# A decoder layer on one core: the last gate cells in a fixed order, their last products by column halves, the last rows' scaling and stores rearranged

## The chip, the core and the metric

The kernel runs on one core of one Trainium2 chip. The metric is device time in microseconds of that core; the time of a kernel is the median of its runs.

## The reference, cut to what matters

One layer of a hybrid decoder (gated linear attention, a short gated convolution, a merge), then a per-layer embedding gate and a final RMSNorm, on 1024 rows of 1024 columns in float32. What the change touches is the end:

```
x = x + merged @ w_out
ple_gate = sigmoid(rms_norm(x, norm_ple_g) @ w_ple_gate)
x = x + ple_gate * (p @ w_ple_proj)
return rms_norm(x, norm_final_g)
```

`rms_norm(x, g)` is `x / sqrt(mean(x*x) + EPS) * g`, row by row. The last line needs the sum of squares of a whole row before any of that row can be scaled.

## The kernel before, in words

**Products.** Every large product is a Strassen-Winograd product on 2x2 quarters, seven products, numbered 0 to 6, for an output of 256 rows by 1024 columns. A `Cell` computes such an output, as two row blocks of 128 rows by two column halves of 512 columns. Each product has four k-tiles of three matmuls (high x high, low x high, high x low parts in fp32r), so 12 matmuls with 512 columns. A cell has three PSUM banks, X, V and Y. Products 0 and 3 go to X, 1 and 5 to V, 2, 4 and 6 to Y (Y begins as a copy of X after product 0). X after product 3 is the output of row block 0, columns 0 to 511; V after product 5 plus a copy of Y after product 2 is row block 0, columns 512 to 1023; Y after product 4 plus a copy of V after product 1 is row block 1, columns 512 to 1023; Y after product 6 is row block 1, columns 0 to 511. `Cell.run(k)` does one product and hands finished quarters to `cons(i, j, src)`, with i the row block and j the column half.

**The last stage.** Four gate cells, gt0 to gt3, one for each pair of row blocks; gt2 makes rows 4 and 5 of eight, gt3 rows 6 and 7. `run_groups(pairs(gts))` lets two cells alternate product by product in the order 0, 1, 2, 3, 5, 4, 6 (`PAIR`); the right-hand sides wg0 to wg6 are resident, and the left-hand operands are sums and differences of tiles loaded from DRAM (`gt2raw` and so on), split into a high part by an ACT cast and a low part by a DVE subtraction. For a finished quarter, `cons` or `piece` does: ACT sigmoid with the row's factor `rg` as scale; DVE product with the quarter's `pe` tile (p @ w_ple_proj, loaded from DRAM); DVE sum onto `x`; ACT square with the row sum as second output (`junk`, then ACT reads the accumulator). When a row's two halves are there, POOL adds the sums and raises them to the power -1/2 (`rf`), and the row is scaled by `rf` and by the gain `gf` (tile `gfin`, the gain broadcast over the partitions) and stored.

**How rows were finished.** Rows 0 to 4 and row 6 go through `cons`: one DVE pass over 1024 columns with factor and gain, one store of 512 KB. Rows 5 and 7 go through `piece` (lines 1671 to 1700): each quarter is multiplied by the gain when its square sum is under way, POOL adds the partial sums (`pre`), and the last piece takes factor and gain together; two stores of 256 KB. For gt3 the last product, 6, is done by column halves (`last_product`, lines 770 to 783): Y is copied to a free bank Z, the first 256 columns are finished in Y, the others in Z, so that the first half's sigmoid runs during the second half's matmuls.

**What sets the order.** `Flow` (lines 257 to 505) records every operation instead of issuing it. `note` gives each a planned cost by engine and size and links it to what it depends on; `set_dues` gives due times; `put_in_order` makes one sequence, in which PE's matmuls keep the order in which they were recorded and the other engines' operations are placed by due time. `emit` issues them all from line 503, which is why every row of the profile says L503; the tiles' names tell the operations apart. Each engine works its own sequence in order, and waits by semaphores for the others. All DMAs are issued by SP.

Of the kernel before, what the change touches and what calls it, by code (L numbers as in the profile page):

```python
# [9 lines left out]
F32 = mybir.dt.float32  # L10
# [246 lines left out]
class Flow:  # L257
# [5 lines left out]
    def __init__(self, tc):  # L263
        nc = tc.nc
        self.tc, self.ops, self.side, self.open, self.hurry, self.bundle = tc, [], True, [], 0.0, None
        self.tensor, self.vector, self.scalar = Port(self, PE, nc.tensor), Port(self, DVE, nc.vector), Port(self, ACT, nc.scalar)
        self.gpsimd, self.sync = Port(self, POOL, nc.gpsimd), Port(self, SP, nc.sync)


    def note(self, engine, op, call, args, kw):  # L270
# [39 lines left out]

# [28 lines left out]
        for v in outs + ins:  # L339
            if isinstance(v, View) and v.buf not in o.bufs:  # L340
# [174 lines left out]
def kernel(  # L515
# [210 lines left out]
    class Cell:  # L726


        def __init__(self, name, side, src, res, cons, prods=ORDER, begin=None, s1=None, u2=None, s5=None, fresh=(), mixed=False):
# [3 lines left out]
            self.s1, self.seed, self.ready, self.halves = s1, None, lambda k: True, None  # L733
            self.raw, self.ring = [None] * 4, {}
            self.steps, self.fresh = ring_steps(name, side, self.raw, fresh, mixed), fresh
# [33 lines left out]

        def last_product(self):  # L770

            other = psm.tile([P, 512], F32, tag=f"m{3 * (1 - self.set)}", name=f"{self.name}Z")
            nc.scalar.copy(other, self.Y)
            self.prep(6)
            shi, slo = self.ring[6]
            rhi, rlo = self.res[6]
            for n, acc in enumerate((self.Y, other)):
                cs = slice(n * 256, n * 256 + 256)
                for kt in range(4):
                    nc.side = False  # L780
                    mm3(acc[:, cs], shi[:, kt, :], slo[:, kt, :], rhi[:, kt, cs], rlo[:, kt, cs], False, kt == 3)
                    nc.side = True
                self.halves(n, acc[:, cs])

        def run(self, k):
# [16 lines left out]
            elif k == 2:  # L802
                self.product(2, self.Y, False)
                self.c12 = self.taken("u2", self.Y)
            elif k == 3:
                self.product(3, self.X, False)
                self.cons(0, 0, self.X)
            elif k == 5:
                self.product(5, self.V, False)
                tt(self.c12, self.V, self.c12, op=ALU.add)  # L810
                self.cons(0, 1, self.c12)
            elif k == 4:
# [3 lines left out]
            elif k == 6 and self.halves:  # L816
                self.last_product()
# [6 lines left out]
    def line_up(groups):  # L824
        for n, g in enumerate(groups):
            for s, c in enumerate(g):
                c.set = (s if len(g) > 1 else n) % 2
        return [(c, k) for g in groups for k in g[0].prods for c in g]

# [774 lines left out]
    with phase("late", [ph["sw"], ep]) as lp:  # L1604
# [56 lines left out]
        with phase("fin", [ph["sw4"]], lp) as gp:  # L1661
# [3 lines left out]
            def make_gate(p, cell):  # L1665
                seen = [0, 0]
                xt, ms, ts, sums = [], [], [None, None], [None, None]

                def piece(i, cs, src, n, done):
                    w = cs.stop - cs.start
                    a = cs.start
                    if a % 512 == 0:
                        ts[i] = gp.tile([P, 512], F32, tag="pe", name=f"pe{p}_{i}_{a}", bufs=4)
                        load(ts[i], ped[2 * p + i][:, a:a + 512])
                    t, xc = ts[i][:, a % 512:a % 512 + w], xt[i][:, cs]
                    act(src, src, AF.Sigmoid, scale=rgate[p, i][:, 0:1])
                    tt(t, src, t, op=ALU.mult)
                    tt(xc, xc, t, op=ALU.add)  # L1680
                    m = gp.tile([P, 1], F32, tag="msl", name=f"msl{p}_{i}_{n}", bufs=4)
                    act(junk[:, 0:w], xc, AF.Square, scale=1.0 / 32.0, accum_out=m)
                    if not done:
                        tt(xc, xc, gf[:, cs], op=ALU.mult)
                        pre = gp.tile([P, 1], F32, tag="pre", name=f"pre{p}_{i}_{n}", bufs=4)
                        nc.gpsimd.tensor_scalar(pre, m, EPS if n == 0 else sums[i][:, 0:1], None, op0=ALU.add)
                        sums[i] = pre
                        return
                    r = sm.tile([P, 1], F32, tag="rstd", name=f"rf{p}_{i}", bufs=4)
                    nc.gpsimd.tensor_scalar(r, m, sums[i][:, 0:1], None, op0=ALU.add)  # L1690
                    nc.gpsimd.tensor_tensor(r, r, mhalf, op=ALU.pow)
                    if a:
                        act(xt[i][:, 512:], xt[i][:, 512:], AF.Copy, scale=r[:, 0:1])
                    else:
                        nc.vector.tensor_scalar(xt[i][:, 512:], xt[i][:, 512:], r[:, 0:1], None, op0=ALU.mult)
                    store(out[rows(2 * p + i), 512:], xt[i][:, 512:])
                    stt(xc, xc, r[:, 0:1], gf[:, cs], op0=ALU.mult, op1=ALU.mult)
                    if a:
                        nc.vector.tensor_scalar(xt[i][:, 0:a], xt[i][:, 0:a], r[:, 0:1], None, op0=ALU.mult)
                    store(out[rows(2 * p + i), 0:512], xt[i][:, 0:512])  # L1700

                def late_cons(i, j, src):
                    if not xt:
                        get()
                    piece(i, slice(512 * j, 512 * j + 512), src, 1 - j, j == 0)

                def halves(n, src):
                    piece(1, slice(256 * n, 256 * n + 256), src, 1 + n, n == 1)

# [102 lines left out]
```

## Time and profile before

| | us |
|---|---|
| median of 3 runs (lowest to highest) | 1082.56 (1082.08 to 1082.73) |
| the profiled execution | 1082.53 |
| its span, first to last instruction | 1080.4 |
| around the span | 2.13 |
| PE busy | 1069.0 |
| start of the last matmul | 1070.26 |
| issue of the last store | 1077.24 |

The mean granted TensorE clock was 0.997. Times in the profile count from the span's start. A row of the timeline gives start, duration, engine, line, operation, output tile <- input tiles, shapes, a count, and in brackets how long the engine had been idle and what released it. PEld is the weight load beside the matmuls, SPq the sequencer of SP that issues DMAs.

### The profile page before, as it was taken

How to read it: one execution, taken by the hardware profiler on the slowest of the kernel's cores; microseconds unless marked ns; L12 is line 12 of the kernel's file. 1: busy time of each engine (PE TensorE's matmuls, PEld its weight loads, DVE VectorE, ACT ScalarE, POOL GpSimd, SP SyncE). 2: the span in 40 equal slices, each digit the busy share in tenths (PEclk: the TensorE clock that was granted, in tenths of full speed). 3: DMA queues.
4: the chain of work that ended last, by engine and by line, in shares of the span. 5: the costliest groups of instructions: out<-in, count | busy, mean ns of one | idle time of the engine just before them, and what ended most of it. 6: DMA issues, size and time to landing. Idle time of an engine off the chain costs nothing.

```text
span 1080.4 us, 14620 instructions
## 1 busy us (share of the span) xinstructions
PE 1069.0 (99%) x4869; PEld 889.4 (82%) x4869; DVE 868.7 (80%) x1341; ACT 602.6 (56%) x1086; POOL 49.2 (5%) x89
## 2 busy tenths in 40 slices
PE   9999999999999999999999999999999999999996
PEld 7887887888888888888888888888888888888885
DVE  6998567679987977857747788887999879889886
ACT  6778538656543455433343367765756635467554
POOL 0000000000000000000000012110000000012013
PEclk9999999999999999999999999999999999999998
DMA  9973564467866597221222779989586779799954
GB/s 324 347 244 105 178 210 136 148 204 231 233 204 222 202 314 260 77 89 49 88 69 69 249 259 326 326 288 334 201 306 214 282 224 313 233 335 326 319 188 156
DMA packets 144827, 239.95 MB, mean 222 GB/s; under 512 B 12016, under 2 KB 57328, under 8 KB 141808
## 3 DMA queue, kind: packets, MB, share of 16 engines
q1 hardware_dynamic: 144752, 239.02, 65.4%
q8 instruction: 38, 0.62, 0.2%
q14 instruction: 37, 0.30, 0.1%
HBM read 158.24 MB, written 80.74 MB: 221 GB/s over the span
## 4 chain that ended last, share of the span: by engine, by line
PE 97%; DVE 1%; ACT 1%; issue 0%; POOL 0%; POOLq 0%; DVEq 0%; ACTq 0%
PE vY L503 3%; PE zaY L503 3%; PE pe L503 2%; PE vX L503 2%; PE zaV L503 2%; PE vV L503 2%; PE op L503 2%; PE zaX L503 2%; PE kv L503 1%; PE ga2Y L503 1%; PE ga0Y L503 1%; PE ga1Y L503 1%; PE cb3Y L503 1%; PE gc1Y L503 1%; PE ga3Y L503 1%; PE gc0Y L503 1%
## 5 line engine op out<-in xcount | busy, mean ns | idle before, releaser
L503 ACT ACTIVATE junk<-x 128x512 bf16<-128x512 f32 (+1 forms) x29 | 17.9, 616 | 18.9 <-DVE x L503 13.9
L503 ACT ACT_TABLE_LOAD x20 | 25.7, 1283 | 1.1 <-PEq L1801 0.7
L503 DVE TENSOR_TENSOR wt<-wt 128x512 f32<-128x512 f32 x32 | 21.6, 685 | 0.3
L503 POOL MEMSET t<- 128x2 f32 x8 | 0.8, 100 | 442.6 <-DMA qkd<-kk 243.7
L503 DVE SCALAR_TENSOR_TENSOR u<-t,vec,u 128x1024 f32<-128x1024 f32 x16 | 20.4, 1281 | 0.0
L503 POOL TENSOR_SCALAR rg<-ms 128x1 f32<-128x1 f32 x8 | 6.6, 822 | 261.2 <-ACT junk L503 261.0
L503 ACT CAST S<-S 128x512 fp32r<-128x512 f32 x14 | 8.7, 619 | 10.0 <-PE op L503 10.0
L503 ACT ACTIVATE og<-op,or 128x256 f32<-128x256 f32 x32 | 13.3, 469 | 1.6 <-POOL or L503 1.6
L503 ACT ACTIVATE oq<-oq,vec 128x512 f32<-128x512 f32 x20 | 13.3, 715 | 0.0
L503 ACT ACTIVATE junk<-op 128x256 bf16<-128x256 f32 x32 | 12.2, 380 | 1.7 <-PE op L503 1.5
L503 PE MATMUL pe<-wpehi,pThi 128*128 128x512 f32 x32 | 12.8, 401 | 0.0
L503 PE MATMUL op<-v,aTh 128*128 128x256 f32 x64 | 12.8, 283 | 0.0
L503 PE MATMUL pe<-wpelo,pThi 128*128 128x512 f32 x32 | 12.8, 399 | 0.0
L503 POOL TENSOR_TENSOR or<-or,mhalf 128x2 f32<-128x2 f32 x16 | 12.7, 795 | 1.3
L503 PE MATMUL pe<-wpehi,pTlo 128*128 128x512 f32 x32 | 12.6, 394 | 0.0
L503 DVE TENSOR_TENSOR szl<-og,szl 128x512 f32<-128x512 f32 x16 | 11.0, 686 | 1.7 <-ACT og L503 1.7
L503 DVE SCALAR_TENSOR_TENSOR S<-S,dds,kv 128x256 f32<-128x256 f32 x24 | 10.4, 475 | 1.9 <-PE kv L503 1.7
L503 DVE SCALAR_TENSOR_TENSOR hq<-hq,vec,rt 128x512 f32<-128x512 f32 x16 | 11.1, 741 | 0.5 <-PE rt L503 0.5
L503 DVE STREAM_TRANSPOSE oT<-szl 128x512 f32<-128x512 f32 x16 | 11.3, 706 | 0.2
L503 DVE TENSOR_TENSOR u<-u,s 128x512 f32<-128x512 f32 x16 | 10.9, 687 | 0.3
L503 DVE TENSOR_TENSOR x<-x,pe 128x512 f32<-128x512 f32 (+1 forms) x17 | 11.0, 656 | 0.2
L503 DVE SCALAR_TENSOR_TENSOR x<-x,rf,gfin 128x1024 f32<-128x1024 f32 (+2 forms) x8 | 8.9, 1114 | 2.7 <-POOL rf L503 2.7
(2908 smaller groups left out, 4103.0 us busy)
## 6 DMA issues: line engine op xcount, KB each, us to landing
wtd<-wt SPq DMA_DIRECT2D x44, 256.0 KB, 3.7
wt<-in_wb_dram SPq DMA_DIRECT2D x8, 1024.0 KB, 7.2
v<-vd SPq DMA_DIRECT2D x16, 512.0 KB, 5.8
wgq<-wtd SPq DMA_DIRECT2D x7, 1024.0 KB, 8.0
qk<-qkd SPq DMA_DIRECT2D x12, 512.0 KB, 5.9
vraw<-in_wv_dram SPq DMA_DIRECT2D x20, 256.0 KB, 4.0
zaraw<-in_wv_dram SPq DMA_DIRECT2D x20, 256.0 KB, 4.0
uq<-ud SPq DMA_DIRECT2D x5, 1024.0 KB, 7.8
```

The source lines that it names most:

```text
L503: o.call(*[place(a) for a in o.args], **{k: place(a) for k, a in o.kw.items()})
```

## The change

1. The planner's cost of an ACT operation with a row sum grows from 0.1 to 0.2 us over a plain one; a DMA issued by an engine other than SP gets a cost of its own. This changes no operation, but the order that the planner makes, in the whole kernel.
2. A new field `hold` makes recorded operations wait, in the plan, for a given earlier operation; `hurry` gives the last quarters' operations an earlier due time.
3. The order of the last two cells' products is written out: gt2's 0, gt3's 0, then gt2: 3, 1, 2; gt3: 3; gt2: 4; gt3: 1; gt2: 5; gt3: 2; gt2: 6; gt3: 5, 4, 6.
4. `by_halves` replaces `last_product`: gt3's products 4 and 6 are both done by column halves, in Y and Z. Z is filled by a copy of half of Y after product 2. Half products of 4 and 6 go through `piece` in four pieces of 256 columns.
5. All of gt2's and gt3's quarters go through `piece`. Rows 4 and 5: each quarter is multiplied by the gain beside its square sum, the row is scaled by two ACT passes and stored whole. Row 6: the same by halves, with two stores; the second gain product and the ACT scaling are held behind steps of row 7. Row 7: its four square sums land in one tile of five columns, `last`, preset to EPS; one DVE reduction adds them, POOL does the power alone; one gain product stands ahead of the reduction, three behind it; then ACT scales columns 512 to 1023 and DVE columns 0 to 511.
6. The partial sums of rows are added by DVE instead of POOL.
7. Row 7's second half is stored by a DMA that ACT issues; all other DMAs stay with SP.

The diff, cut to its core:

```diff
-            o.cost = 0.10 + n * 0.000833 + (0.1 if "accum_out" in kw else 0.0)
+            o.cost = 0.10 + n * 0.000833 + (0.2 if "accum_out" in kw else 0.0)
...
+        if op == "dma_start" and engine != SP:
+            o.cost, o.lat = 0.1, 2.3 + shape[0] * n * 4 / 250e3
...
+        if self.hold is not None:
+            preds[self.hold] = max(preds.get(self.hold, 0.0), 0.0 if self.ops[self.hold].engine == engine else 0.08)
...
-        def last_product(self):
-            other = psm.tile([P, 512], F32, tag=f"m{3 * (1 - self.set)}", name=f"{self.name}Z")
-            nc.scalar.copy(other, self.Y)
-            self.prep(6)
...
+        def by_halves(self, k):
+            self.prep(k)
+            shi, slo = self.ring[k]
+            rhi, rlo = self.res[k]
+            for n, acc in enumerate((self.Y, self.Z)):
                 cs = slice(n * 256, n * 256 + 256)
                 for kt in range(4):
                     nc.side = False
                     mm3(acc[:, cs], shi[:, kt, :], slo[:, kt, :], rhi[:, kt, cs], rlo[:, kt, cs], False, kt == 3)
                     nc.side = True
-                self.halves(n, acc[:, cs])
+                if k == 4:
+                    tt(self.c22[:, cs], acc[:, cs], self.c22[:, cs], op=ALU.add)
+                    self.halves(1, n, self.c22[:, cs])
+                else:
+                    self.halves(0, n, acc[:, cs])
...
                 self.c12 = self.taken("u2", self.Y)
+                if self.halves:
+                    self.Z = psm.tile([P, 512], F32, tag=f"m{3 * (1 - self.set)}", name=f"{self.name}Z")
+                    nc.scalar.copy(self.Z[:, 256:], self.Y[:, 256:])
...
+                    if p == 3 and i:
+                        if not times:
+                            sums[1] = gp.tile([P, 5], F32, tag="last", name="last")
+                            nc.gpsimd.memset(sums[1], EPS)
+                        m = sums[1][:, n:n + 1]
...
+                    if p == 3 and i:
+                        times.append((cs, t, added))
+                        if not done:
+                            return
+                        nc.vector.tensor_reduce(pre, sums[1], mybir.AxisListType.X, ALU.add)
+                        summed = len(nc.ops) - 1
+                    else:
+                        if p < 3 or not done:
+                            tt(xc, xc, gf[:, cs], op=ALU.mult)
+                        nc.vector.tensor_scalar(pre, m, EPS if n == 0 else sums[i][:, 0:1], None, op0=ALU.add)
                         sums[i] = pre
...
+                    for n, (cs, to, _) in enumerate(times if done else ()):
+                        nc.hold = (times[2][2], summed)[n] if n < 2 else len(nc.ops) - 1
+                        tt(to, xt[i][:, cs], gf[:, cs], op=ALU.mult)
+                    nc.hold = None
+                    if done:
+                        r = sm.tile([P, 1], F32, tag="rstd", name=f"rf{p}_{i}", bufs=4)
+                        nc.gpsimd.tensor_tensor(r, pre, mhalf, op=ALU.pow)
+                        if p == 3 and i == 0:
+                            rest.append(r)
+                            return
+                        if p < 3:
+                            for b in (0, 512):
+                                act(xt[i][:, b:b + 512], xt[i][:, b:b + 512], AF.Copy, scale=r[:, 0:1])
+                            store(out[rows(2 * p + i), :], xt[i])
+                            return
+                        act(xt[1][:, 512:], ts[1, 1], AF.Copy, scale=r[:, 0:1])
+                        nc.vector.tensor_scalar(xt[1][:, 0:512], ts[1, 0], r[:, 0:1], None, op0=ALU.mult)
+                        store(out[rows(7), 0:512], xt[1][:, 0:512])
+                        nc.scalar.dma_start(out[rows(7), 512:], xt[1][:, 512:])
+                        for q, late in enumerate((made, squared)):
+                            js = slice(512 * q, 512 * q + 512)
+                            xj = xt[0][:, js]
+                            if q:
+                                nc.hold = added
+                                tt(xj, xj, gf[:, js], op=ALU.mult)
+                            nc.hold = late
+                            act(xj, xj, AF.Copy, scale=rest[0][:, 0:1])
+                            nc.hold = None
+                            store(out[rows(6), js], xj)
...
+                def halves(j, n, src):
+                    a = 512 * j + 256 * n
+                    nc.hurry = 1.0
+                    piece(1, slice(a, a + 256), src, 2 * (1 - j) + n, a == 256)
+                    nc.hurry = 0.0
...
-                    if i == 1 and p >= 2:
+                    if p >= 2:
                         return late_cons(i, j, src)
...
-            run_groups(pairs(gts))
+            last = pairs(gts)
+            gts[2].order = [(0, 0), (1, 0), (0, 3), (0, 1), (0, 2), (1, 3), (0, 4), (1, 1),
+                            (0, 5), (1, 2), (0, 6), (1, 5), (1, 4), (1, 6)]
+            run_groups(last)
```

More of the change, by code (lines that the diff above doesn't have):

```diff
@@ L733, in __init__ @@
             self.s1, self.seed, self.ready, self.halves = s1, None, lambda k: True, None
-            self.raw, self.ring = [None] * 4, {}
+            self.raw, self.ring, self.order = [None] * 4, {}, None
             self.steps, self.fresh = ring_steps(name, side, self.raw, fresh, mixed), fresh
@@ L811, in run @@
                 self.cons(0, 1, self.c12)
+            elif k in (4, 6) and self.halves:
+                self.by_halves(k)
             elif k == 4:
@@ L827, in line_up @@
                 c.set = (s if len(g) > 1 else n) % 2
-        return [(c, k) for g in groups for k in g[0].prods for c in g]
+        return [(g[s], k) for g in groups
+                for s, k in (g[0].order or [(s, k) for k in g[0].prods for s in range(len(g))])]
     def single(cs):
@@ L1678, in piece @@
                     act(src, src, AF.Sigmoid, scale=rgate[p, i][:, 0:1])
+                    made = len(nc.ops) - 1
                     tt(t, src, t, op=ALU.mult)
                     tt(xc, xc, t, op=ALU.add)
-                    m = gp.tile([P, 1], F32, tag="msl", name=f"msl{p}_{i}_{n}", bufs=4)
-                    act(junk[:, 0:w], xc, AF.Square, scale=1.0 / 32.0, accum_out=m)
[L1683 to L1686, printed above, removed]
-                        sums[i] = pre
-                        return
@@ L1689, in piece @@
[L1689 to L1700, printed above, removed]
+                    added = len(nc.ops) - 1
+                    if p == 3 and i:
[4 more added lines that the diff above has]
+                    else:
+                        m = gp.tile([P, 1], F32, tag="msl", name=f"msl{p}_{i}_{n}", bufs=4)
```

23 lines of the change are left out of this document (10 added, 13 removed).

## The prediction, made before the result

> **What bounds the kernel now.** I read the page first (its first part), then the list of waits of PE, then busy time by stretch:
>
> ```profile
> PE 1069.0 (99%) x4869; PEld 889.4 (82%) x4869; DVE 868.7 (80%) x1341; ACT 602.6 (56%) x1086; POOL 49.2 (5%) x89
> ```
> ```profile
> PE warm L503 <- DVE zero L503: 1.4, 1, 1.4
> ```
> ```profile
> core 0 of [0], span 1080.4 us
> core 0: us, PE busy (x) PEld busy (x) DVE busy (x) ACT busy (x) POOL busy (x), PEclk, DMA share, GB/s
> 1032.00:1060.00 28.00, 28.00 (x125) 23.21 (x124) 20.53 (x30) 13.12 (x27) 3.33 (x4) 1.00 0.54 197
> 1060.00:1070.50 10.50, 10.50 (x58) 9.02 (x56) 9.41 (x15) 6.74 (x15) 3.75 (x5) 1.00 0.50 175
> 1070.50:1080.40 9.90, 0.04 (x1) 0.00 (x0) 4.97 (x11) 3.11 (x10) 4.87 (x6) 0.72 0.28 106
> ```
>
> PE waits once, 1.4 us at the start, and is then busy without a gap until 1070.5 us: 1069.0 + 1.4 + 9.9 makes the span. So three things can change the time: more or fewer matmuls, a wait of PE, and the 9.9 us in which PE has finished and the last rows are still normalized and stored. The timeline of that tail, by engine: PE (first and last matmul of gt2's product 5, then the last of each half of gt3's product 6), ACT, DVE, POOL and SP's queue:
>
> ```profile
> 1053.91 0.39 PE L503 MATMUL gt2V<-wg5hi,gt2hi 128*128 128x512 f32 x1
> ```
> ```profile
> 1056.40 0.39 PE L503 MATMUL gt2V<-wg5hi,gt2lo 128*128 128x512 f32 x1
> ```
> ```profile
> 1068.82 0.28 PE L503 MATMUL gt3Y<-wg6hi,gt3lo 128*128 128x256 f32 x1
> ```
> ```profile
> 1070.26 0.28 PE L503 MATMUL gt3Z<-wg6hi,gt3lo 128*128 128x256 f32 x1
> ```
> ```profile
> 1070.80 0.43 ACT L503 ACTIVATE gt3Z<-gt3Z,rg 128x256 f32<-128x256 f32 x1
> 1071.16 0.62 ACT L503 ACTIVATE junk<-x 128x512 bf16<-128x512 f32 x1
> 1071.68 0.19 ACT L503 ACTIVATION_READ_ACCUMULATOR junk<-x 128x1 f32 x1
> 1071.90 0.42 ACT L503 ACTIVATE junk<-x 128x256 bf16<-128x256 f32 x1
> 1072.23 0.19 ACT L503 ACTIVATION_READ_ACCUMULATOR junk<-x 128x1 f32 x1
> 1073.35 0.42 ACT L503 ACTIVATE junk<-x 128x256 bf16<-128x256 f32 x1 [0.93 <-DVE x L503]
> 1073.67 0.19 ACT L503 ACTIVATION_READ_ACCUMULATOR junk<-x 128x1 f32 x1
> 1076.07 0.72 ACT L503 ACTIVATE x<-x,rf 128x512 f32<-128x512 f32 x1 [2.21 <-POOL rf L503]
> ```
> ```profile
> 1071.87 0.42 DVE L503 TENSOR_TENSOR pe<-gt3Z,pe 128x256 f32<-128x256 f32 x1
> 1072.20 0.69 DVE L503 TENSOR_TENSOR x<-x,gfin 128x512 f32<-128x512 f32 x1
> 1072.80 0.43 DVE L503 TENSOR_TENSOR x<-x,pe 128x256 f32<-128x256 f32 x1
> 1073.14 0.43 DVE L503 TENSOR_TENSOR x<-x,gfin 128x256 f32<-128x256 f32 x1
> 1074.45 0.49 DVE L503 TENSOR_SCALAR x<-x,rf 128x512 f32<-128x512 f32 x1 [0.89 <-POOL rf L503]
> ```
> ```profile
> 1072.12 1.51 POOL L503 TENSOR_SCALAR rf<-msl,pre 128x1 f32<-128x1 f32 x1
> 1073.61 0.28 POOL L503 TENSOR_SCALAR pre<-msl,pre 128x1 f32<-128x1 f32 x1
> 1073.85 0.56 POOL L503 TENSOR_TENSOR rf<-rf,mhalf 128x1 f32<-128x1 f32 x1
> 1074.41 0.57 POOL L503 TENSOR_SCALAR rf<-msl,pre 128x1 f32<-128x1 f32 x1
> 1075.06 0.97 POOL L503 TENSOR_TENSOR rf<-rf,mhalf 128x1 f32<-128x1 f32 x1
> ```
> ```profile
> 1076.81 0.81 SPq L503 DMA_DIRECT2D out_dram<-x  x2
> ```
>
> From the last matmul's start (1070.26, my zero) the last row goes through sigmoid, product with pe, sum onto x, square sum, POOL add, POOL power, scaling, store. Three places lose time. Z's product stands behind others on DVE (sigmoid done at 1071.23, product at 1071.87). A gf product of another row (1072.20) delays the sum onto x to 1072.80. And POOL is late: the last square sum is read by 1073.86, but POOL takes row 5's power first (1073.85), adds row 7's sum at 1074.41, and its power lasts until 1076.03. The first store of the last pair leaves at 1076.81, **6.55 us** after zero; 3.59 us later the span ends.
>
> **The change part by part.** Its own time is the profiled execution's, 1082.53 us: span 1080.4 and 2.13 around it, 0.03 under the median of the runs. Positions come from comparing the instruction order of both programs.
>
> *Matmuls.* Product 4 of gt3 is 24 matmuls of 256 columns in place of 12 of 512. Twelve starts of 512 take (1056.40 - 1053.91)/11 = 0.226 us each, those of 256 (1070.26 - 1068.82)/12 = 0.12. 24 x 0.12 - 12 x 0.226 = **+0.15 us**, all on PE, which nothing hides.
>
> *Fixed order.* gt2's products 3 and 4 come 10.9 us earlier, gt2's 6 and gt3's 3 come 5.4 earlier, gt3's 1 and 2 come 10.9 later. Their operands are split by one ACT cast and one DVE subtraction each. The raw tiles are loaded well before (rival 4), so I take 0. The tightest place is new: gt3's product 6 may not write its first half before DVE has read product 4's. The chain to it is told by gt2's add behind its product 5:
>
> ```profile
> 1056.83 0.69 DVE L503 TENSOR_TENSOR gt2u<-gt2V,gt2u 128x512 f32<-128x512 f32 x1 [1.10 <-PE gt2V L503]
> ```
>
> The last matmul of gt3's product 5 starts at -5.87 (47 x 0.12 + 0.226 back). DVE's add starts 0.43 later (1056.40 to 1056.83) and lasts 0.69, until -4.75; sigmoid 0.72 (the scaling's row), pe product 0.60 from start to start (1072.20 to 1072.80), half add 0.42, and 0.03 at each of two handovers: -2.95. PE wants it at -2.76 (23 x 0.12). 0.2 us of cover: 0 taken, up to 0.3 in the range.
>
> *Planner cost of squares, hurry, hold.* They change no instruction, but reorder ACT, DVE, SP and a few PE instructions all through the kernel (groups of 1 to 3 matmuls change places in four stretches). PE has no gap to lose there: 0 taken; for the range -0.1 to +0.4, a quarter of the one wait that the trace shows (an estimate).
>
> *Sums.* Seven POOL adds go; six 128x1 adds and one 128x5 reduction come to DVE, none shown in that size or form. The nearest rows are ACT's 128x1 read of 0.19 and, above, DVE's 256-wide product of 0.42; below, nothing. I take 0.19. Only the reduction is on the path.
>
> *Rows 4 to 6.* Row 4's 1.28 us pass on DVE becomes two gf products there and two ACT scalings of 0.72; rows 5 and 6 likewise. ACT pays for it: it was busy 6.74 of 10.5 us before the end and is now nearly full. Row 5's factor: DVE adds gt3u until -4.75, then come that sum and a 512 gf product, until -4.0, and POOL's power runs beside the product. How a power fares there, and how ACT's 512-wide passes follow each other, is told by
>
> ```profile
> 999.24 0.69 DVE L503 TENSOR_TENSOR gt0S<-gt0raw,gt0raw 128x512 f32<-128x512 f32 x1
> 999.84 0.69 DVE L503 TENSOR_TENSOR gt1S<-gt1raw,gt1raw 128x512 f32<-128x512 f32 x1
> ```
> ```profile
> 999.49 0.85 POOL L503 TENSOR_TENSOR rg<-rg,mhalf 128x1 f32<-128x1 f32 x1
> ```
> ```profile
> 1067.21 0.71 ACT L503 ACTIVATE gt3s<-gt3s,rg 128x512 f32<-128x512 f32 x1
> 1067.82 0.64 ACT L503 ACTIVATE gt2Y<-gt2Y,rg 128x512 f32<-128x512 f32 x1
> ```
>
> The power, 0.56 alone (1073.85), ended here 0.41 after the DVE operation that it met (999.93), though another followed at once. So row 5's factor comes at -3.6. From there ACT is packed: three 512 scalings at 0.61 (1067.21 to 1067.82), four 256 sigmoids at 0.36 (1070.80 to 1071.16), one 512 square at 0.74 (1071.16 to 1071.90), three 256 squares at 0.53 (256 columns, 0.21, less), the last with its read 0.51 (1073.35 to 1073.86): 1.83 + 1.44 + 0.74 + 1.59 + 0.51 = 6.1, and 0.1 for handovers (1073.23 to 1073.35): 6.2. The last square is in at **+2.6**, against +3.6 before. Beyond ACT's queue stand row 6's scaling, which waits for its own factor (DVE sum at about -1, power by 0), and both squares behind it.
>
> *Behind the sum.* Reduction until +2.8; the first of three gf products starts with its end (the start of one operation is 0.1 ahead of the end of the one before: 1072.80 in 1072.89), at +2.75, and ends at +3.2; power at +3.6; ACT scaling 0.72 and handovers: **+4.4**. (The Trainium skill, page "SBUF — State Buffer", section "Who interferes with whom", speaks against these products standing there: a DVE instruction with two SBUF inputs and a GpSimd instruction that reads SBUF exclude each other, and the later one waits for the whole of the earlier. By it the power loses 0.25 us against one beside an idle DVE; the row at 999.49 agrees, 0.85 against 0.56, while the add of 1.51 at 1072.12 lasted longer than one operation, see rival 2.) DVE: three products (0.34 from 1072.80 to 1073.14, 0.34, 0.43) until +3.86, scaling 0.49: +4.4. Both last stores leave at +4.4 instead of +6.55.
>
> *Stores.* Row 7's second half is issued by ACT, which issued no DMA before: no row shows it. The nearest are SP's six stores of the tail, and the DMA engines' busy tenths from 1074 to 1081 us in slices of 0.175:
>
> ```profile
> DMA to landing us min/median/max: 2.0/2.2/2.7
> ```
> ```profile
> DMA  0000000000699999992029999999700000000000
> ```
>  I take SP's, bounds -0.1 and +0.7. That the two leave together brings nothing against SP's two in a row: the last pair's data fill the DMA engines without a gap for eight slices, 1.4 us. (The Trainium skill, page "DMA: Bandwidth & Descriptors", section "Issuing engines are not separate DMA queues", says that all issuers share the same DMA engines and a second issuer saves issue time alone. If issue were the limit, that would be 0.4 here, half of the 0.81 of two issues, and 1080.1; the row of busy tenths shows the data as the limit.) Row 6's second store leaves near +3.4, is through 1.5 later, and so is out of the way. So 3.59 us from first issue to the end stay.
>
> Sum: 0.15 + (4.4 - 6.55) = -2.0: 1082.53 - 2.0 = **1080.5 us**.
>
> **Rivals.**
> 1. *ACT is not packed and the power is not held up.* Z's sigmoid then starts 0.43 after the last matmul, as DVE's add did at 1056.83; 0.36 + 0.61 + 0.53 + 0.51 put the last square at +2.45; with the reduction of 0.19, a free power of 0.56 and 0.72 ACT's store leaves at +3.95: 0.45 less, 1080.1. For it: POOL's spans vary. Against: the count above.
> 2. *The power waits for all three gf products.* The POOL add at 1072.12 was stuck through three products, until 1073.63. Then the power ends at +3.86 + 0.42, the stores leave at +4.8 (DVE's half) and +5.05 (ACT's) in place of +4.4: 0.4 to 0.7 more, 1081.1. Against it stands the row at 999.49, an instruction of the same kind as the power.
> 3. *ACT's store lands late*, by the spread of landings, 0.7: 1081.2.
> 4. *Slower: PE waits for an operand in the fixed order.* One order for PE means that a late split stops everything. Place: gt2's product 3, now at 1037.6. If none of the four products pulled forward had its split ready, PE would wait 4 x (0.72 + 0.69) = 5.6 us, an ACT and a DVE pass each: 1086.1. The sign turns at 2.0 us of waiting. Against it stands the last load of a gt2 tile,
>
> ```profile
> 1018.32 1.14 SPq L503 DMA_DIRECT2D gt2raw<-gd  x1
> ```
>
> 18 us ahead, and that ACT was busy only 13.12 of the 28 us from 1032, DVE 20.53.
>
> **How the numbers follow.** A measurement of this kernel tells about 0.2% (2.2 us) from no change, so the line lies at 1080.4, inside my forecast's own spread of 1080.1 to 1080.9. Forecast 0.47, rival 1 0.22, rivals 2 and 3 0.12 each, rival 4 0.06, the rest 0.01. Faster: rival 1 and 0.18 of the forecast, 0.40. Slower: rival 4, 0.06. Same: 0.54. The range goes from 1079.7 (rival 1, and 0.3 from a cheaper DVE chain or landing) to 1081.9 (rivals 2 or 3 with 0.7 of PE wait, reordering or both together).
>
> **What would show it.** PE without a gap, last matmul near 1070.4. The last square read 2.6 us after it (2.3: rival 1). The last power about 0.7 long, ending within a gf product (over 1.2: rival 2). First store of the last pair 4.4 after zero, the end 3.6 later (over 4.2: rival 3). A wait of PE on DVE or ACT above 0.3 us, at gt2X or at gt3Y's last product, would make the prediction wrong (rival 4), and so would a last matmul more than 0.5 from 1070.4.

## The result and the profile after

| | before | after |
|---|---|---|
| median (22 runs each) | 1082.15 us | 1080.74 us |
| lowest to highest | 1081.70 to 1082.95 | 1080.12 to 1081.62 |
| the profiled execution | 1082.53 | 1080.98 |
| its span | 1080.4 | 1079.2 |

After over before is 0.9986, 95% interval 0.998 to 0.9992: 1.4 us less, 0.13%, inside the 0.2% that the prediction took as its line. The forecast was 1080.5 (-2.0), the range 1079.7 to 1081.9.

The page's first part and PE's list of waits, after. PE again waits once, at the start:

```profile
PE 1069.8 (99%) x4881; PEld 890.8 (83%) x4881; DVE 868.8 (81%) x1353; ACT 605.5 (56%) x1095; POOL 45.5 (4%) x83
```
```profile
PE warm L507 <- DVE zero L507: 1.4, 1, 1.4
```

Busy time by stretch, after (PE, PEld, DVE, ACT, POOL with counts, then PEclk, DMA share, GB/s). The first line is a stretch of the prediction; the second begins where PE is nearly done:

```profile
1060.00:1070.50 10.50, 10.50 (x68) 9.56 (x67) 7.76 (x17) 7.87 (x17) 2.00 (x3) 1.00 0.28 107
1070.50:1079.20 8.70, 0.85 (x8) 0.65 (x6) 4.77 (x13) 4.41 (x13) 1.21 (x2) 0.80 0.37 144
```

ACT took over work of DVE ahead of the end (6.74 to 7.87 us busy from 1060 to 1070.5, DVE 9.41 to 7.76). POOL has 1.21 us left at the end where it had 4.87. The timeline of the tail, after: the last matmul, then ACT, DVE, POOL and the queues.

```profile
1071.07 0.28 PE L507 MATMUL gt3Z<-wg6hi,gt3lo 128*128 128x256 f32 x1
```
```profile
1071.67 0.43 ACT L507 ACTIVATE gt3Z<-gt3Z,rg 128x256 f32<-128x256 f32 x1
...
1073.54 0.19 ACT L507 ACTIVATION_READ_ACCUMULATOR junk<-x 128x1 f32 x1
...
1074.69 0.72 ACT L507 ACTIVATE x<-pe,rf 128x512 f32<-128x512 f32 x1 [0.21 <-DMA out_dram<-x]
1075.44 0.41 ACTq L507 DMA_DIRECT2D out_dram<-x  x1
```
```profile
1067.74 0.42 DVE L507 TENSOR_TENSOR gt3s<-gt3Y,gt3s 128x256 f32<-128x256 f32 x1
...
1072.25 0.42 DVE L507 TENSOR_TENSOR pe<-gt3Z,pe 128x256 f32<-128x256 f32 x1
1072.70 0.42 DVE L507 TENSOR_TENSOR x<-x,pe 128x256 f32<-128x256 f32 x1
...
1073.76 0.16 DVE L507 TENSOR_REDUCE pre<-last 128x1 f32<-128x5 f32 x1
1073.83 1.08 DVE L507 TENSOR_TENSOR pe<-x,gfin 128x256 f32<-128x256 f32 x3
1075.03 0.49 DVE L507 TENSOR_SCALAR x<-pe,rf 128x512 f32<-128x512 f32 x1
```
```profile
1066.54 0.93 POOL L507 TENSOR_TENSOR rf<-pre,mhalf 128x1 f32<-128x1 f32 x1 [3.57 <-DVE pre L507]
...
1074.06 0.60 POOL L507 TENSOR_TENSOR rf<-pre,mhalf 128x1 f32<-128x1 f32 x1 [2.95 <-DVE pre L507]
```
```profile
1075.54 0.33 SPq L507 DMA_DIRECT2D out_dram<-x  x1
```

From the last matmul's start (1071.07) the last square is in at +2.66, the power done at +3.59, the first store of the last pair out at +4.37 (ACT's) and the second at +4.47 (SP's); the span ends at +8.12, where it was +10.14 before (1070.26 to 1080.4). The tail so gave 2.02 us. Of that, 0.81 went again, because the last matmul starts later: 1071.07 against 1070.26. Two matmuls split that: the first of gc3pX on h3 (early) and the first of gt2X (where the last cells begin). Before, then after:

```profile
70.50 0.39 PE L503 MATMUL gc3pX<-h3hi,gc3phi 128*128 128x512 f32 x1
...
1032.15 0.39 PE L503 MATMUL gt2X<-wg0hi,gt2hi 128*128 128x512 f32 x1
```
```profile
70.94 0.39 PE L507 MATMUL gc3pX<-h3hi,gc3phi 128*128 128x512 f32 x1
...
1032.81 0.39 PE L507 MATMUL gt2X<-wg0hi,gt2hi 128*128 128x512 f32 x1
```

Up to the first one 0.44 us is lost, between them (called D below: 961.65 and 961.87) 0.22, and from gt2X to the last matmul (called the gate: 38.11 and 38.26) 0.15. Only the last was in the prediction's sum.

### The profile page after: what moved, and what is told of

Read it like the earlier page. It is cut to its first block, busy times and chain, and to the rows that moved or that the text cites. A ratio compares the mean times of both kernels' runs of the same rounds, so it can differ in the third digit from the quotient of the medians.

```text
span 1079.2 us, 14643 instructions
## 1 busy us (share of the span) xinstructions
PE 1069.8 (99%) x4881; PEld 890.8 (83%) x4881; DVE 868.8 (81%) x1353; ACT 605.5 (56%) x1095; POOL 45.5 (4%) x83
## 4 chain that ended last, share of the span: by engine, by line
PE 98%; ACT 1%; DVE 0%; issue 0%; POOL 0%; ACTq 0%; DVEq 0%
PE vY L507 3%; PE zaY L507 3%; PE pe L507 2%; PE vX L507 2%; PE zaV L507 2%; PE vV L507 2%; PE op L507 2%; PE zaX L507 2%; PE kv L507 1%; PE ga2Y L507 1%; PE ga0Y L507 1%; PE ga1Y L507 1%; PE ga3Y L507 1%; PE cb3Y L507 1%; PE gc0Y L507 1%; PE xc1Y L507 1%
## 5 line engine op out<-in xcount | busy, mean ns | idle before, releaser
L507 ACT ACTIVATE wt<-wt,vec 128x512 f32<-128x512 f32 x16 | 10.5, 715 | 0.6 <-issue 0.6
```

The costliest lines, as they stand in the source:

```text
L507: o.call(*[place(a) for a in o.args], **{k: place(a) for k, a in o.kw.items()})
```

## The experiments

Each of e1 to e12 ran in five rounds beside before. In the expectations, "the first matmul of gc3pX" is the one on h3 shown above. The table gives what the profiles say: the start of that matmul, D, the gate, then, from the last matmul, the first store of the last pair, and from that store to the end of the span. Times are in us; the last five columns are of the profiled execution.

| kernel | median | before beside it | ratio, 95% | gc3pX | D | gate | store | to the end |
|---|---|---|---|---|---|---|---|---|
| before | 1082.15 | | | 70.50 | 961.65 | 38.11 | 6.55 | 3.59 |
| after | 1080.74 | 1082.15 | 0.9986, 0.998 to 0.9992 | 70.94 | 961.87 | 38.26 | 4.37 | 3.75 |
| e1 | 1080.60 | 1082.29 | 0.9984, 0.9975 to 0.9993 | 70.33 | 961.62 | 38.42 | 4.53 | 3.72 |
| e2 | 1080.65 | 1082.29 | 0.9985, 0.9977 to 0.9994 | 70.86 | 961.83 | 38.26 | 4.37 | 3.59 |
| e3 | 1081.86 | 1082.29 | 0.9995, 0.9987 to 1.0004 | 71.03 | 961.88 | 39.85 | 4.01 | 3.76 |
| e4 | 1081.99 | 1082.29 | 0.9997, 0.9988 to 1.0006 | 71.11 | 961.85 | 38.29 | 4.79 | 4.49 |
| e5 | 1082.23 | 1082.68 | 0.9996, 0.9987 to 1.0005 | 70.71 | 961.61 | 38.42 | 5.59 | 3.89 |
| e6 | 1080.95 | 1082.68 | 0.9983, 0.9974 to 0.9992 | 70.72 | 961.64 | 38.26 | 4.39 | 3.74 |
| e7 | 1081.19 | 1082.68 | 0.9984, 0.9975 to 0.9992 | 71.75 | 961.84 | 38.26 | 4.85 | 3.60 |
| e8 | 1080.50 | 1082.68 | 0.9978, 0.9969 to 0.9988 | 70.62 | 961.67 | 38.26 | 4.38 | 3.58 |
| e9 | 1080.85 | 1082.42 | 0.9985, 0.9977 to 0.9994 | 70.84 | 961.84 | 38.27 | 4.37 | 3.74 |
| e10 | 1080.30 | 1082.42 | 0.9981, 0.9972 to 0.9989 | 70.26 | 961.62 | 38.27 | 4.37 | 3.58 |
| e11 | 1081.00 | 1082.42 | 0.9988, 0.998 to 0.9997 | 70.55 | 961.87 | 38.26 | 4.84 | 3.72 |
| e12 | 1082.61 | 1082.42 | 1.0, 0.9991 to 1.0009 | 70.79 | 961.84 | 38.11 | 6.54 | 3.60 |

The intervals are about 1.9 us wide, so most steps below can't be told apart by times. D, the gate and the two tail columns repeat to 0.05 us between executions of one order (after and e9, e8 and e10), and the verdicts rest on them. The theory at this point was that every term of the prediction's sum held, and that the planner's cost added 0.2 us of PE; the rival, that the late PE is chance.

### e1: the planner's cost as before

```diff
-            o.cost = 0.10 + n * 0.000833 + (0.2 if "accum_out" in kw else 0.0)
+            o.cost = 0.10 + n * 0.000833 + (0.1 if "accum_out" in kw else 0.0)
```

> The kernel after, with the planner's cost of an ACT operation with row sum at 0.1 again, all else kept. Measure: D, from the first matmul of gc3pX (70.50 before, 70.94 after) to the first of gt2X (1032.15 and 1032.81), so 961.65 before and 961.87 after. Theory: the planner's new order costs PE 0.2 us where zp's matmuls change places with vX's (75 to 100 us), and the other 0.44 of the late PE arises in the first 8 us, where PE steps to full speed at another moment in each execution. Then D falls to 961.65, the tail stays (first store of the last pair 4.4 after the last matmul), and the time is 0.2 below after: 1080.5. Rival, as the prediction had it: the reordering costs PE nothing; D stays 961.87 and the time 1080.7.

D fell to 961.62, as the theory said. But the tail didn't stay: the gate grew by 0.16 and the store came 0.16 later. PE's rows show where, after first (the last matmul of product 4 and the first of product 6), then e1 with one row more:

```profile
1068.20 0.28 PE L507 MATMUL gt3Z<-wg4hi,gt3lo 128*128 128x256 f32 x1
1068.32 0.28 PE L507 MATMUL gt3Y<-wg6hi,gt3hi 128*128 128x256 f32 x1
```
```profile
1067.34 0.28 PE L507 MATMUL gt3Z<-wg4hi,gt3lo 128*128 128x256 f32 x1
1067.51 0.39 PE L507 MATMUL gt3Y<-wg6hi,gt3hi 128*128 128x256 f32 x1
1067.74 0.28 PE L507 MATMUL gt3Y<-wg6lo,gt3hi 128*128 128x256 f32 x1
```

After goes on every 0.12; e1 is held for 0.05 and then 0.11 at product 6, right after DVE's half add:

```profile
1065.71 0.21 DVE L507 TENSOR_SCALAR pre<-msl,pre 128x1 f32<-128x1 f32 x1 [0.23 <-ACT junk L507]
...
1067.04 0.42 DVE L507 TENSOR_TENSOR gt3s<-gt3Y,gt3s 128x256 f32<-128x256 f32 x1
```

This is the place that the prediction called the tightest. In e1's order DVE idles 0.23 us for ACT's square before row 5's sum, and the cover is gone. So the new cost is two things at once: 0.25 dearer ahead of the last cells, 0.3 cheaper in them.

### e6 and e12: the two things apart

e6 gives the new cost to the last stage alone (a flag set where its pool opens); e12 is the kernel before with the new cost everywhere.

```diff
-            o.cost = 0.10 + n * 0.000833 + (0.2 if "accum_out" in kw else 0.0)
+            o.cost = 0.10 + n * 0.000833 + ((0.2 if self.late else 0.1) if "accum_out" in kw else 0.0)
...
+            nc.late = True
```

> The kernel after, with the planner's cost of a square 0.2 over a plain operation in the last stage alone and 0.1 before it. Theory: the new cost does two things, a reordering of 75 to 100 us that costs PE 0.2 us, and a better order of the last 40 us, which e1 had lost (last matmul 0.16 later behind gt2X's first, first store of the last pair 4.53 after it in place of 4.37). So here D is 961.62 as in e1, and gt2X's first to the last matmul 38.27 and the tail 4.37 as in after: 0.2 to 0.3 below after, 1080.4 to 1080.5, if PE's step to full speed falls in the same place. Rival: the tail of e1 was another execution's jitter; then D falls here too, but the last stage varies by the same 0.16 without a cause.

> The kernel before, with the planner's cost of a square 0.2 over a plain operation, nothing else. Theory: D rises from 961.65 to 961.87 as in after, since the same matmuls change places between 75 and 100 us; the rest of PE and the tail (6.55 to the first store of the last pair) stay: 0.2 above before. Rival: the 0.2 of after came from its other changes; D stays 961.65.

In the profile both came out as the theory said. e6 has the low D of e1 (961.64), and the gate and tail of after (38.26, 4.39), so e1's tail was no jitter. e12 has the D of after (1032.63 - 70.79 = 961.84), with before's gate and tail unchanged. The time of e6, 1080.95, doesn't show its 0.2 (1080.4 to 1080.5 was expected if the start of the kernel fell alike), and e12's 0.2 above before is inside its interval; by the profile the price of the reordering is 0.2 us of PE, repeated in seven profiles (e2, e3, e4, e7, e9, e11, e12 at 961.83 to 961.88, all with the new cost everywhere) against five without it ahead of the last cells (e1, e5, e6, e8, e10, at 961.61 to 961.67).

Where the 0.2 goes can be read from the starts of the matmuls: nearly all of it is lost at one matmul of `zp`, about 25 us after gc3pX. PE's rows around it, before and then e12:

```profile
95.22 0.39 PE L503 MATMUL vX<-v3hi,h3hi 128*128 128x512 f32 x1
95.45 0.40 PE L503 MATMUL zp<-low,g 128*128 128x512 f32 x1
95.69 0.39 PE L503 MATMUL vX<-v3lo,h3hi 128*128 128x512 f32 x1
```
```profile
95.96 0.39 PE L503 MATMUL vX<-v3hi,h3lo 128*128 128x512 f32 x1
96.29 0.51 PE L503 MATMUL zp<-low,g 128*128 128x512 f32 x1
96.63 0.39 PE L503 MATMUL vX<-v3hi,h3hi 128*128 128x512 f32 x1
```

Before, the two steps around it take 0.23 and 0.24, the usual pace; in e12 they take 0.33 and 0.34. PE waits there, and for ACT. The weight load of this matmul has the wait, again before and then e12:

```profile
95.34 0.19 PEld L503 LDWEIGHTS zp<-low,g 128*128 128x128 f32 x1 [0.15 <-ACT t L503]
```
```profile
96.28 0.19 PEld L503 LDWEIGHTS zp<-low,g 128*128 128x128 f32 x1 [0.36 <-ACT t L503]
```

The ACT pass that it waits for (`t<-zp`, which reads an earlier `zp`) ends 0.07 after the start of the preceding matmul before, and 0.27 after it in e12, where the new order has put a cast ahead of that pass. In the six profiles without the new cost there (before, e1, e5, e6, e8, e10) the weight load idles 0.14 to 0.16 us and the two steps take 0.46 to 0.47 together; in the eight with it, 0.35 to 0.37 and 0.65 to 0.67. PE's list of waits has no line for this, because a matmul's row is drawn 0.39 long while the next one starts 0.23 later: a delay of up to 0.16 leaves no idle time between rows. e1's hold at product 6 is missing from that list for the same reason.

### e2: row 7's second half stored by SP

```diff
-                        nc.scalar.dma_start(out[rows(7), 512:], xt[1][:, 512:])
+                        nc.note(ACT, "dma_start", tc.nc.sync.dma_start, (out[rows(7), 512:], xt[1][:, 512:]), {})
```

The operation keeps its place in the plan; SP issues it.

> The kernel after, with row 7's second half stored by a DMA of SP, at the same place of the plan, in place of ACT's. Theory: the store issued by ACT lands late (2.7 us from issue against 2.0 for SP's), and the data of the last pair are the limit, so two issues in a row from SP cost nothing: from the first issue of the last pair to the end 3.6 us in place of 3.76, and the time 0 to 0.2 lower, 1080.6. Rival: two issues in a row on SP put the second one 0.4 later, and it ends the span: 4.1 us from first issue to end, 1081.1.

First store of the last pair at 4.37, as after; then 3.59 to the end in place of 3.75: the theory. The last pair in the DMA views, after (from 1075 us on) and then e7 (from 1076.5), whose edit is told below (KB each, us to landing):

```profile
out_dram<-x ACTq DMA_DIRECT2D x1, 256.0 KB, 2.7
out_dram<-x SPq DMA_DIRECT2D x1, 256.0 KB, 2.8
```
```profile
out_dram<-x SPq DMA_DIRECT2D x1, 256.0 KB, 2.0
out_dram<-x ACTq DMA_DIRECT2D x1, 256.0 KB, 2.5
```

In after SP's own store, 0.10 behind ACT's, lands as late as ACT's. In e2 SP's two issues take 0.81 together, and the second still lands sooner than the last one of after. So the second issuer saves nothing here, and in after's form it costs 0.16. That ACT as issuer is the cause isn't shown: in e7 ACT issues too, but 0.24 behind SP, and 3.60 pass from the first store to the end, as in e2. After's pair differs in leaving only 0.10 apart and in ACT going first; no run took these two apart.

### e3: product 4 whole

```diff
-            elif k in (4, 6) and self.halves:
+            elif k == 6 and self.halves:
                 self.by_halves(k)
             elif k == 4:
                 self.product(4, self.Y, False)
                 tt(self.c22, self.Y, self.c22, op=ALU.add)
-                self.cons(1, 1, self.c22)
+                if self.halves:
+                    self.Z = psm.tile([P, 512], F32, tag=f"m{3 * (1 - self.set)}", name=f"{self.name}Z")
+                    nc.scalar.copy(self.Z[:, 256:], self.Y[:, 256:])
+                    for n in range(2):
+                        self.halves(1, n, self.c22[:, n * 256:n * 256 + 256])
+                else:
+                    self.cons(1, 1, self.c22)
```

> The kernel after, with gt3's product 4 done whole (12 matmuls of 512 columns), its output then finished in the same two pieces of 256, Z copied after it. Theory: PE saves 0.15 us of matmuls, but gt3's product 6 may not write Y before DVE has added it: a wait of about 0.43 + 0.42 + 0.03 - 0.23 = 0.65 us on DVE at gt3Y, and the four pieces' sigmoids crowd behind it, so that the last matmul comes 0.5 later and the last store 0.5 to 1.0 later: 1081.2 to 1081.7. Rival: the halves of product 4 bring nothing, since ACT's queue sets the last square in any case: PE 0.15 less and the same tail, 1080.6.

PE waits 1.47, not 0.65, and not for DVE:

```profile
1069.49 0.36 ACT L507 COPY gt3Z<-gt3Y 128x256 f32<-128x256 f32 x1
...
1069.91 0.39 PE L507 MATMUL gt3Y<-wg6hi,gt3hi 128*128 128x256 f32 x1 [1.47 <-ACT gt3Z L507]
```

The copy of Z has to read Y before product 6 writes it, and it stands on ACT behind row 5's scalings and a square. The expectation had left the copy out. The gate is 1.58 longer than in after, the store 0.36 sooner after the last matmul, so 1.2 is lost; the time is 1.1 above after, more than expected. In this order of products the halves, with the early copy of Z that belongs to them, save a wait of 1.5 us for 0.15 of PE.

### e4: no order written out

```diff
-            gts[2].order = [(0, 0), (1, 0), (0, 3), (0, 1), (0, 2), (1, 3), (0, 4), (1, 1),
-                            (0, 5), (1, 2), (0, 6), (1, 5), (1, 4), (1, 6)]
```

> The kernel after, without the order written out: the last two cells alternate as before (gt2's product 6 stands between gt3's 4 and 6). Theory: rows 4 and 5 then finish 2.8 us before the end instead of 8.4, and row 5's last quarter (sigmoid 0.61, square 0.74, two scalings 1.22 on ACT) falls into the tail where ACT is packed, while 1.4 of product 4's pieces leave it: the last square and the last store come about 1 us later, 1081.7, PE without a wait. Rival: the order is worth nothing, 1080.7 and the first store of the last pair 4.4 after the last matmul.

The size was right (the tail 9.28 against 8.12, the time 1.25 above after), but only a part of it lies where it was expected. The first store of the last pair is 0.42 later, from ACT's queue. Two scalings stand there between row 7's squares; the first is row 6's, as in after, and the second is row 5's first half, which POOL's power for row 5 has let go at 1073.06:

```profile
1072.33 1.49 ACT L507 ACTIVATE x<-x,rf 128x512 f32<-128x512 f32 x2
1073.72 0.40 ACT L507 ACTIVATE junk<-x 128x256 bf16<-128x256 f32 x1
```

The other 0.74 lies behind that store: row 5's 512 KB leave among the last ones, and all of these land later. From 1072 us on, e4 (median us to landing):

```profile
out_dram<-x SPq DMA_DIRECT2D x3, 256.0 KB, 2.7
out_dram<-x SPq DMA_DIRECT2D x1, 512.0 KB, 2.7
out_dram<-x ACTq DMA_DIRECT2D x1, 256.0 KB, 3.3
```

### e5 and e11: the sums from both sides

e5 is the kernel before with the sums of rows 5 and 7 on DVE; e11 is after with every sum on POOL.

```diff
-                        nc.gpsimd.tensor_scalar(pre, m, EPS if n == 0 else sums[i][:, 0:1], None, op0=ALU.add)
+                        nc.vector.tensor_scalar(pre, m, EPS if n == 0 else sums[i][:, 0:1], None, op0=ALU.add)
...
-                    nc.gpsimd.tensor_scalar(r, m, sums[i][:, 0:1], None, op0=ALU.add)
+                    nc.vector.tensor_scalar(r, m, sums[i][:, 0:1], None, op0=ALU.add)
```

> The kernel before, with the partial sums of rows 5 and 7 added by DVE in place of POOL (which keeps the powers), all else as before. Theory: the adds on POOL are the largest part of the gain, since the one of row 5 is stuck for 1.51 us behind DVE products, row 7's comes after row 5's power, and its power ends 2.2 us after the last square. With them on DVE the last power ends about 1.5 sooner, and the first store of the last pair leaves 4.9 to 5.2 after the last matmul in place of 6.55: 1080.9 against 1082.3. Rival: DVE is the bound of the tail, and the sums wait in its queue behind 512-wide products: less than 0.5 is gained, 1081.8, and the rest of the gain came from the rearranged products.

> The kernel after, with every partial sum of rows 4 to 7 added by POOL again (row 7's four, one after another, in place of DVE's reduction). Theory: e5 gave 0.96 of the 2.2 us by which the first store of the last pair came sooner, so the adds on POOL should cost about as much here: row 7's last add 0.5 to 0.6 on POOL in place of 0.16 and a handover, and an add or two stuck behind DVE products; first store of the last pair 5.0 to 5.5 after the last matmul, 1081.4 to 1081.9. Rival: what made POOL late before was two rows' sums at the same time; with row 5 done 4 us sooner its adds cost only their own length, 0.3: 1081.0.

e5 moved the store from 6.55 to 5.59, not to 5.2 or less, and gave part of it back: PE's gate is 0.31 longer (product 6 held at gt3Y, as in e1), and with four stores within 1.6 us the end comes 3.89 after the store. The rival was nearer, and the time (1082.23, 0.45 below before beside it and inside the interval) gained less than either said. POOL's row says what was left: both rows' powers, one behind the other, the first with 0.93, and row 7's ends at 1075.26 though DVE had its sum by 1074.42:

```profile
1073.77 1.49 POOL L503 TENSOR_TENSOR rf<-rf,mhalf 128x1 f32<-128x1 f32 x2 [7.86 <-DVE rf L503]
```
```profile
1074.21 0.21 DVE L503 TENSOR_SCALAR rf<-msl,pre 128x1 f32<-128x1 f32 x1
```

e11's store came at 4.84, 0.47 later than in after: 0.16 short of the theory's 5.0 and 0.17 above the rival's 0.3, so between the two. Its rows: an add stuck behind a DVE product, then the last add, which the power (0.57) follows.

```profile
1072.80 0.83 POOL L507 TENSOR_SCALAR pre<-msl,pre 128x1 f32<-128x1 f32 x1 [0.81 <-ACT junk L507]
```
```profile
1073.73 0.58 POOL L507 TENSOR_SCALAR pre<-msl,pre 128x1 f32<-128x1 f32 x1
```

The time, 1081.00, is the rival's, 0.15 above e9 on the same chip. So the sums alone are worth 0.5 (in after) to 0.96 (in before) of the 2.18 by which the store came sooner. The order is worth 0.42 of it (e4), the late gain products 0.48 (e7). What the reduction in one piece and the scalings on ACT are worth, no run took apart. The parts overlap and don't add.

### e7: row 7's gf products ahead of its sum

```diff
                     for n, (cs, to, _) in enumerate(times if done else ()):
-                        nc.hold = (times[2][2], summed)[n] if n < 2 else len(nc.ops) - 1
                         tt(to, xt[i][:, cs], gf[:, cs], op=ALU.mult)
```

> The kernel after, without the hold on row 7's gf products: all four stand ahead of the reduction on DVE, each behind its quarter's sum. Theory: two of them fall between the last quarters' products on DVE and delay the last sum onto x by about 0.35, the last one stands ahead of the reduction with 0.34, and the power, then beside an idle DVE, gains 0.04: the last factor comes 0.6 later, the stores 0.6 later, 1081.3. Rival, the Trainium skill's exclusion of DVE and GpSimd (page SBUF, Who interferes with whom) at its full price of one product, 0.25 us or more: the power gains 0.25 to 0.4 and takes back most of it; 1080.9.

The power beside an idle DVE took 0.55 (0.60 in after):

```profile
1075.60 0.55 POOL L507 TENSOR_TENSOR rf<-pre,mhalf 128x1 f32<-128x1 f32 x1 [3.79 <-DVE pre L507]
```

It ends at +4.30 in place of +3.59, 0.7 later. That speaks for the theory, whose 0.04 gained is 0.05, and against the rival at 0.25. The time from the end of the reduction to the start of the power, 0.14, is the same in both. The first store comes 0.48 later, but the end only 0.33: the two stores leave 0.24 apart and not 0.10, and 3.60 pass to the end in place of 3.75.

### e8, e9 and e10: a version with both gains, and after again

e8 and e10 are e6 with the edit of e2; e9 is after unchanged.

> e6 and e2 together: the new cost in the last stage alone, and row 7's second half stored by SP. Theory: both gains add, 0.25 of PE and 0.16 of the last pair's landing: D 961.62, first issue to end 3.59, about 0.4 below after: 1080.3. Rival: within what the executions vary by (0.6 us in the moment of PE's step to full speed) nothing is seen in the time; only the profile's differences show it.

> The kernel after, unchanged, on the chip on which e10 to e12 run, as their yardstick. Theory: 1.4 below before; first store of the last pair 4.37 after the last matmul, 3.75 to the end, D 961.87; the first matmul of gc3pX on h3 anywhere between 70.3 and 71.8, which is what executions of one kernel differ by. Rival: the place of that matmul belongs to the kernel; then it is 70.94 again, as in the first profile of after.

> e8 again, beside after on one chip. Theory: 0.4 below after (0.25 of PE, 0.16 of the last pair's landing), its profile D 961.6, 4.38 and 3.59. Rival: the same time as after within 0.2.

The gains add in the profile (D 961.67 and 961.62, 3.58 to the end), and the medians, 1080.50 and 1080.30, are the lowest of all. On one chip e10 is 0.55 below after (e9: 1080.39 to 1081.36; e10: 1079.88 to 1080.77); the single times overlap, so the profile, and not the times, says that it is the theory's 0.4. e9 repeats after's D, gate and tail to 0.03, and its gc3pX comes at 70.84 where it was 70.94.

## Why the prediction was right, and where it wasn't

**Matmuls.** +0.15 on PE: the gate grew from 38.11 to 38.26. Right. (By the two rounded figures that the prediction shows, 24 x 0.12 - 12 x 0.226, it would be 0.17.)

**Fixed order and its tightest place.** No PE wait, as said. DVE's half add ended at 1068.16, 2.91 ahead of the last matmul (forecast 2.95), and PE wanted it at 1068.32. The cover was real and thin: e1 lost it through an idle 0.23 us on DVE. (e5, in the order of before, lost the like: a 1.28 us scaling pass that had waited 0.77 for POOL's factor stood ahead of the half add.)

**Sums.** The reduction, taken as 0.19, took 0.16. As a term it was right; e11 and e5 put the sums at 0.5 to 0.96 of the gain.

**Rows 4 to 6.** Row 5's power ended at 1067.47, 3.60 ahead of the last matmul, as forecast. The last square is in at +2.66 (forecast +2.6), though ACT isn't alone in it: Z's sigmoid starts at +0.60, and from there DVE's product and sum take until 1073.12, right ahead of the last square. ACT's queue and DVE's reach that square within 0.1 us of each other, so the packed ACT alone doesn't set it.

**Behind the sum.** Reduction done at +2.84 (forecast +2.8), power at +3.59 (+3.6), stores out at +4.37 and +4.47 (+4.4). The rival in which the power waits for all three products is out: they end at 1074.91, the power at 1074.66. The row that the forecast used held: the power ended 0.41 after the DVE operation that it met, at 1067.47 for row 5 (the gain product ahead of it ended at 1067.06) and at 1074.66 for row 7 (the first of the three ended at 1074.25). What this costs was read too high: against e7's idle DVE the power loses 0.05 and not 0.25, since the 0.14 from the reduction to POOL's start, which the forecast did not count, is paid in both cases. The sum came out because the end of the DVE product set it. (The Trainium skill, page "SBUF — State Buffer", section "Who interferes with whom", has the later of the two wait for the whole of the earlier; the row of 0.93 at 1066.54 against 0.55 in e7 agrees, and in after's last power nearly all of the wait is hidden.)

**Stores.** 3.59 was forecast from first issue to the end, 3.75 measured. e2 gives 3.59 exactly, so the 0.16 belongs to the way in which after issues the pair, not to ACT as issuer (e7: 3.60). The rival of a late landing had the landing right (2.7 against 2.0) and the effect wrong: 0.16 and not 0.7, since the second of SP's two stores lands late as well.

**Planner cost.** This is the step that failed: "0 taken", on the ground that PE has no gap to lose. PE does wait in the reordered part, where the list of its waits has no line: the weight load of one `zp` matmul idles 0.35 us for ACT in place of 0.15, and the matmuls behind it start 0.2 later (e6 and e12; D grew by 0.22). The value lies within the bound of 0.4 that was given.

**The sum.** 0.15 + 0.22 on PE and -2.02 in the tail make -1.65. Around the span, after's runs take 1.8 us on average (1.75 to 1.84), before's beside e9 to e12 2.0 (1.84 to 2.16): another -0.2 that the prediction had not, cause open. The medians give -1.41, on e9's chip -1.57, so 0.3 to 0.4 of this gain is not seen in the times, and no run says why; the start of the kernel, which moves single executions by up to 1.5, may hold it. The two profiled executions differ there by 0.44, the wrong way.

**What was luck.** The time ended 0.24 above the forecast, but the gain, 1.41, is 0.6 short of the 2.0 that was forecast: the forecast started from one execution of before, 1082.53, and the median of 22 is 1082.15. One of the prediction's own signs of being wrong came true as well: the last matmul started at 1071.07, more than 0.5 from 1070.4. Of these 0.67, 0.44 are the start and 0.22 the planner's cost; PE showed no wait in the last cells, which that sign was meant for.

## What to carry to other kernels

When the bound engine is full to its last instruction, read the tail as one chain from that instruction and price each link by a row; the forecast here hit every point up to the stores to 0.1 us. A list of waits without a line doesn't say that PE never waits: matmul rows overlap, so look at the distance from start to start, and at the waits of the weight load. A cost in a planner is an edit of the whole program: compare the distance between two fixed matmuls far apart, which repeats to 0.05 us, and not the times, which vary by 1 us. Move a row's end out of the tail before speeding its parts: the sums alone gave less than half (e5) while another row's power and stores stood in the same place.

## What the runs showed of the hardware

The first matmuls run at half pace, and the step to full pace falls at another moment in each execution. PE's rows there, of after:

```profile
6.72 0.63 PE L507 MATMUL pe<-wpehi,pThi 128*128 128x512 f32 x1
7.15 0.51 PE L507 MATMUL pe<-wpelo,pThi 128*128 128x512 f32 x1
7.50 0.39 PE L507 MATMUL pe<-wpehi,pTlo 128*128 128x512 f32 x1
```

From start to start a matmul takes 0.43 before the step and 0.23 behind it; the 0.35 from 7.15 to 7.50 holds the step. The step falls between 4.6 and 7.5 us in the fourteen profiles, and the first of gc3pX on h3 between 70.26 and 71.75; in e7, the latest, a wait of 0.49 for an ACT cast comes on top. Until 33 us every engine issues the same operations in the same order in all fourteen, and from 37 us to gc3pX PE takes 33.79 in each. So 70.94 against 70.50 comes from the execution and not from the change: it was chance. (The Trainium skill, page "TensorE: Matmul & The Clock Gate", section "Part 1: The HAM clock gate (the "warmup" mystery)", says that the clock steps up after a busy window that runs free of the kernel's start, so that the moment varies from run to run by some 0.5 us either way. That it varies, the rows show; by how much differs, since 4.6 to 7.5 us is wider.) PEclk shows 1.00 in that stretch too, so the granted clock doesn't tell of it; the starts do.
